# Up projection of two of three token blocks by Strassen's seven products, in a second pass over the weights

## The chip, the cores and the metric

The kernel runs on one core of a Trainium2 chip. The metric is device microseconds (us) of one execution. A core has TensorE (PE, matmuls; PEld are its weight loads), VectorE (DVE), ScalarE (ACT), GpSimd (POOL) and SyncE (SP), which here only issues transfers. TensorE accumulates into PSUM, of which the kernel uses eight tiles of 128 x 512 float32; the other engines compute on SBUF and PSUM, GpSimd on SBUF alone.

## What is computed

One step of a layer of a streaming encoder: attention, a state-space layer, then a gated feed-forward network with a causal convolution of width 3 over positions. The change touches the last part alone:

```
f, conv_state = _conv_ffn(_rmsnorm(h, g_ffn_norm), conv_hist, p)     # returned: h + f

def _conv_ffn(xn, conv_hist, p):
    up = xn @ p["w_up"]                      # (1024 + 8*16, 1024) @ (1024, 2*2816)
    full = concatenate([conv_hist, up], axis=1)
    conv = w[0] * full[:, 0:S] + w[1] * full[:, 1:S + 1] + w[2] * full[:, 2:S + 2] + p["b_dw"]
    gate, val = conv[..., :D_FF], conv[..., D_FF:]
    y = (silu(gate) * val) @ p["w_down"]     # (., 2816) @ (2816, 1024)
```

There are 1024 prompt positions and 8 running streams of 16 positions, 1152 tokens in all.

## The kernel before

Everything is held transposed: channels on the 128 partitions, tokens along the row. The 1152 tokens are three blocks of TB = 384 (b = 0, 1, 2); block 2 has the last 256 prompt tokens and the 128 tokens of the running streams. The 2816 channels of the hidden layer are NF = 22 column tiles of 128 (i), each with a gate and a value half.

Matmuls are of float32r operands (32 bit, fewer bits of mantissa). So every operand is split in a high part `h` (ScalarE, `acopy`) and a low part `l` (VectorE: source minus high part), and each product is three matmuls: hi.hi, lo.hi, hi.lo (`mm3`). One matmul has a 128x128 weight and 384 columns.

`phase_de` computes h into `hT` (all blocks, in SBUF), its norm, and the split normed input `hnh`, `hnl` of each block. Then, for every tile i and block b: `up(i, b)` accumulates gate and value in a PSUM tile `pu` each (8 x 3 matmuls); ScalarE copies `pu` to `u` and starts the convolution `c`; VectorE adds the two other taps (line 123); silu, product and split give `act`. `down(i, b, m)` multiplies `act` with one of eight 128-column pieces of the tile's `w_down` into a PSUM tile `pd`, which VectorE adds into `hT` (line 105). The downs of tile i - 1 are put one by one between the matmuls of tile i (`fill`). A weight tile (128x1024) is loaded once (`ws`), split into `wh` and `wl`, and serves all three blocks. `pu` has four PSUM tiles in turn, `pd` four.

The order of each engine's instructions is set by a scheduler that works on a model of the machine; each engine then runs its list in order. The loads stand in SP's list, also in order.

Of the kernel before, what the change touches and what calls it, by code (L numbers as in the profile page):

```python
# [72 lines left out]
SD0, SD1 = 12, 3  # L73


def build(tc, t):
# [4 lines left out]
    with root:  # L81
# [51 lines left out]
        def mm3(out, pairs, first=True, last=True):  # L133
            n = 3 * len(pairs)
            i = 0
            for (wh, wl), (xh, xl) in pairs:
                for w, x in ((wh, xh), (wl, xh), (wh, xl)):
                    nc.tensor.matmul(out, lhsT=w, rhs=x, start=first and i == 0, stop=last and i == n - 1)  # L138
                    i += 1
# [38 lines left out]
        q_dram = dram.tile([SEQ, H * QD], F32, name="q_dram")  # L178

# [1178 lines left out]
        def phase_de():  # L1358
# [4 lines left out]
            with left, right:  # L1363
                next(c_steps)
                wA = right.enter_context(tc.tile_pool(name="wA", bufs=3, side="right", **L))
# [13 lines left out]
                wB = right.enter_context(tc.tile_pool(name="wB", bufs=3, side="right", **L))  # L1379
# [42 lines left out]
                for n, closed in enumerate(c_steps):  # L1422
                    next(sd, None)
                    if closed:
                        if so is None:
                            for _ in sd:
                                pass
                            blp[2] = right.enter_context(tc.tile_pool(name="bl2", bufs=1, side="right", **L))
                            so = osteps(2)
# [17 lines left out]
                def wout(ms, b, o):  # L1447
                    pw = {}
# [19 lines left out]

                def norm(b):
# [26 lines left out]
                for n, b in enumerate(order):  # L1496
                    hload(b)
# [21 lines left out]
                def up(i, b, fill):  # L1519
                    res = []  # L1520
                    for gv in range(2):
                        hi, lo = W[i][gv]
                        f = gv * NF + i
                        w = [cv[:, f, z:z + 1] for z in range(4)]
                        p_ = psum("u", [P, TB], "pu")
                        for k in range(8):
                            mm3(p_, [((hi[:, k * P:(k + 1) * P], lo[:, k * P:(k + 1) * P]), (hn[b][0][:, k], hn[b][1][:, k]))],
                                first=k == 0, last=k == 7)
                            if k % 2 == 1:
                                fill()  # L1530
                        c = wk("M", [TB], "c")
                        nc.scalar.activation(out=c, in_=p_, func=AF.Identity, scale=w[2], bias=w[3])  # L1532
                        n = min(TB, SEQ - b * TB)
                        u = wk("M", [2 + 2 + TB + 2 * NB], "u")
                        if b == 0:
                            nc.gpsimd.memset(u[:, 0:2], 0.0)
                        else:
                            nc.gpsimd.tensor_copy(out=u[:, 0:2], in_=halo[i, gv][:, TB:TB + 2])  # L1538
                        acopy(u[:, 2:2 + n], p_[:, 0:n])
                        halo[i, gv] = u  # L1540
                        for z in (1, 0):
                            stt(c[:, 0:n], u[:, z:z + n], w[z], c[:, 0:n], ALU.mult, ALU.add)
                        if n < TB:
                            us = u[:, 2 + n:2 + n + NB * (DSEQ + 2)].rearrange("p (b s) -> p b s", b=NB)
# [42 lines left out]
                for i, b in seq:  # L1587
# [13 lines left out]
                    while todo:  # L1601
                        fill()
# [130 lines left out]
```

## Time and profile before

| | |
|---|---|
| three runs | 1546.43, 1547.09, 1541.39 us; median 1546.43 |
| profiled execution | 1542.52 us, its span 1540.5 us, instructions 23789 |
| mean granted TensorE clock | 0.973 of full speed |
| TensorE busy over the span | 1469.7 us (95%), 8733 matmuls |
| VectorE, ScalarE, GpSimd busy | 1099.0 (71%), 678.7 (44%), 324.5 us (21%) |
| transfers | 122.15 MB, mean 79 GB/s |

The span is the time from the first to the last instruction of the profiled execution; that execution took 2 us more than its span. Shares over the whole span mix the attention stages with the feed-forward stage, which takes the second half of it (from some 700 us on). In a row "x528" is a count of instructions, the number after a comma the mean duration of one in ns.

### The profile page before, as it was taken

What the parts mean: (1) busy time and instruction counts of PE and PEld (TensorE: products, weight loads), DVE (VectorE), ACT (ScalarE), POOL (GpSimd) and SP (SyncE); (2) the same over time, 40 slices, a digit from 0 to 9 for tenths busy, and PEclk for the clock granted to TensorE, in tenths of its full rate; (3) what the DMA queues carried; (4) which work ended last, traced back from release to release, by engine and by line L of the source; (5) the groups of instructions that cost most, each with busy time, mean ns of one, the idle gap of its engine ahead of it and who ended that gap; (6) DMA issues with size and microseconds to landing.
All of it is one profiled execution on the core that took longest, in us unless ns stands there. A gap on an engine that the chain in (4) does not pass through costs nothing.

```text
span 1540.5 us, 23789 instructions
## 1 busy us (share of the span) xinstructions
PE 1469.7 (95%) x8733; PEld 1415.3 (92%) x8733; DVE 1099.0 (71%) x2327; ACT 678.7 (44%) x1315; POOL 324.5 (21%) x624
## 2 busy tenths in 40 slices
PE   6989759999999999999999999999999999999998
PEld 6969647787789999999999999999999999999998
DVE  8876997575878864677676777777777677776766
ACT  6334266666567875345233333333333333333321
POOL 3271872310645221121100000000000000000000
PEclk9989859999899999999999999999999999999999
DMA  7384244733221323620121111111111111111103
GB/s 205 96 245 128 91 159 85 244 78 97 86 66 57 95 70 122 194 83 2 43 76 44 45 42 42 42 42 42 42 42 42 42 42 41 42 42 42 41 1 134
DMA packets 93460, 122.15 MB, mean 79 GB/s; under 512 B 39204, under 2 KB 73124, under 8 KB 92356
## 3 DMA queue, kind: packets, MB, share of 16 engines
q1 hardware_dynamic: 92960, 120.44, 26.1%
q8 instruction: 68, 1.11, 0.3%
q14 instruction: 48, 0.39, 0.1%
q0 software_dynamic: 384, 0.20, 0.1%
HBM read 93.95 MB, written 26.65 MB: 78 GB/s over the span
## 4 chain that ended last, share of the span: by engine, by line
PE 78%; DVE 8%; DMA 4%; POOL 4%; ACT 3%; issue 2%; SPq 1%; DVEq 0%; ACTq 0%; POOLq 0%
PE pu L138 36%; PE pd L138 17%; PE pw L138 7%; PE pk L138 2%; PE up L138 2%; POOL w L105 1%; PE pq L138 1%; PE po L1262 1%; PE psm L1217 1%; PE pst L1250 1%; PE pst L1249 1%; PE pst L1251 1%; PE po L1260 1%; PE po L1261 1%; PE pg L138 1%
## 5 line engine op out<-in xcount | busy, mean ns | idle before, releaser
L105 DVE TENSOR_TENSOR hT<-hT,pd 128x384 f32<-128x384 f32 x528 | 287.9, 550 | 218.7 <-PE pd L138 218.5
L138 PE MATMUL pu<-hnh,wh 128*128 128x384 f32 x1056 | 356.6, 338 | 0.0
L138 PE MATMUL pu<-hnl,wh 128*128 128x384 f32 x1056 | 356.4, 338 | 0.0
L138 PE MATMUL pu<-hnh,wl 128*128 128x384 f32 x1056 | 356.1, 337 | 0.0
L138 PE MATMUL pd<-act,wh 128*128 128x384 f32 x1056 | 348.7, 336 | 0.5 <-DVE hT L105 0.4
L1532 ACT ACTIVATE c<-pu,cvh 128x384 f32<-128x384 f32 x132 | 88.6, 671 | 309.8 <-PE pu L138 309.6
L138 PEld LDWEIGHTS pd<-act,wh 128*128 128x128 f32 x1056 | 197.7, 188 | 2.4 <-DVE hT L105 2.3
L138 PEld LDWEIGHTS pu<-hnh,wh 128*128 128x128 f32 x1056 | 198.4, 188 | 0.0
L138 PEld LDWEIGHTS pu<-hnl,wh 128*128 128x128 f32 x1056 | 198.3, 188 | 0.0
L138 PEld LDWEIGHTS pu<-hnh,wl 128*128 128x128 f32 x1056 | 198.0, 188 | 0.0
L123 DVE SCALAR_TENSOR_TENSOR c<-u,cvh,c 128x256 f32<-128x256 f32 (+1 forms) x352 | 171.0, 516 | 26.8 <-ACT u L102 14.2
L138 PE MATMUL pd<-act,wl 128*128 128x384 f32 x528 | 177.4, 336 | 0.0
L102 ACT ACTIVATE act<-c 128x384 fp32r<-128x384 f32 x66 | 34.7, 525 | 158.0 <-DVE c L105 158.0
L1538 POOL COPY u<-u 128x2 f32<-128x2 f32 x88 | 19.9, 227 | 384.4 <-DVE c L105 174.0
L138 PEld LDWEIGHTS pd<-act,wl 128*128 128x128 f32 x528 | 99.2, 188 | 0.0
L105 DVE TENSOR_TENSOR wl<-ws,wh 128x1024 fp32r<-128x1024 f32 x74 | 92.0, 1248 | 7.9 <-ACT wh L102 7.9
L102 ACT ACTIVATE wh<-ws 128x1024 fp32r<-128x1024 f32 x74 | 77.9, 1057 | 14.8 <-PE pw L138 8.4
L1550 POOL COPY cvo<-u 128x2 f32<-128x2 f32 x44 | 8.1, 184 | 355.2 <-ACT u L102 355.2
L1554 ACT ACTIVATE c<-c 128x384 f32<-128x384 f32 x66 | 34.6, 525 | 74.7 <-DVE c L123 74.6
L102 ACT ACTIVATE u<-pu 128x384 f32<-128x384 f32 (+2 forms) x176 | 66.3, 404 | 0.0
L138 PE MATMUL pw<-oh,wh 128*128 128x384 f32 x192 | 65.0, 340 | 0.2 <-DVE ql L123 0.2
L138 PE MATMUL pw<-oh,wl 128*128 128x384 f32 x192 | 64.4, 336 | 0.0
(461 smaller groups left out, 3088.5 us busy)
## 6 DMA issues: line engine op xcount, KB each, us to landing
ws<-in_w_up SPq DMA_DIRECT2D x44, 512.0 KB, 3.6
ws<-in_w_down SPq DMA_DIRECT2D x22, 512.0 KB, 3.7
xs<-in_xT SPq DMA_DIRECT2D x24, 192.0 KB, 3.3
os<-o_dram SPq DMA_DIRECT2D x24, 192.0 KB, 3.1
hT<-in_xT SPq DMA_DIRECT2D x24, 192.0 KB, 4.4
out_yT<-hT SPq DMA_DIRECT2D x24, 192.0 KB, 2.1
cf<-in_cT SPq DMA_DIRECT2D x8, 512.0 KB, 7.8
cn<-in_cn SPq DMA_DIRECT2D x8, 512.0 KB
```

The lines of the kernel that those rows point to most:

```text
L102: nc.scalar.activation(out=out, in_=in_, func=AF.Copy, scale=scale)
L105: (eng or nc.vector).tensor_tensor(out=out, in0=a, in1=b, op=op)
L123: nc.vector.scalar_tensor_tensor(out=out, in0=a, scalar=s, in1=b, op0=op0, op1=op1)
L138: nc.tensor.matmul(out, lhsT=w, rhs=x, start=first and i == 0, stop=last and i == n - 1)
L1217: nc.tensor.matmul(p_[:, u, 0:n], lhsT=qh[0:r, h, z * P:(z + 1) * P], rhs=kT[jj][0][0:r, 4 * g + h, 0:n], start=True, stop=True)
L1249: nc.tensor.matmul(o_, lhsT=kh[0:r, 4 * g + h, ks], rhs=qh[0:r, h, qs_], start=True, stop=False)
L1250: nc.tensor.matmul(o_, lhsT=kl[:, 4 * g + h, ks], rhs=qh[0:QD, h, qs_], start=False, stop=False)
L1251: nc.tensor.matmul(o_, lhsT=kh[0:QD, 4 * g + h, ks], rhs=ql[:, h, qs_], start=False, stop=True)
L1260: nc.tensor.matmul(po[:, qs_], lhsT=vhs, rhs=ph[:, sc_], start=f, stop=False)
L1532: nc.scalar.activation(out=c, in_=p_, func=AF.Identity, scale=w[2], bias=w[3])
L1538: nc.gpsimd.tensor_copy(out=u[:, 0:2], in_=halo[i, gv][:, TB:TB + 2])
L1554: nc.scalar.activation(out=g_, in_=g_, func=AF.Silu)
```

## The change

Blocks 1 and 2 no longer get a plain up projection. Write one tile's weights as a 2 x 2 matrix of halves, A11 and A12 for the gate (input channels 0 to 511, 512 to 1023), A21 and A22 for the value, and the normed input as B11, B21 (block 1, the two halves of the channels) and B12, B22 (block 2). The four results of A times B are eight half products; Strassen's scheme in Winograd's form needs seven, of sums of the A's (S1 to S4) and of the B's (T1 to T4), and adds the products up. Sums of the products fall partly in PSUM (three tiles per column tile, A, Y and Z: products that are needed together accumulate in one), partly on VectorE.

There are now two passes over the tiles:

- Pass 1: block 0 as before (`up1`, with its downs). Meanwhile `bsteps` reads h of blocks 1 and 2 back from a DRAM buffer `h_dram`, scales it by the norm and makes and splits the seven B operands, a step of 15 VectorE instructions of 192 columns every two tiles.
- Pass 2: `up2` computes blocks 1 and 2. The up weights are loaded and split again, as halves of 512 columns (`hw`); S1 to S4 are made first, by GpSimd (`sx`). The down weights are loaded and split again too.

In both passes the low part of every weight half is made by GpSimd (`half`). `hT` is replaced by `h0` (block 0, pass 1) and `y12` (blocks 1 and 2, loaded from `h_dram` at the start of pass 2 into space that held block 0). The downs queue in one list `todo` and run six behind (LAG). Copies of the convolution's edges, on GpSimd before, are on ScalarE in pass 2.

```diff
@@ new constants
+NX, NW, NA, NN = 8, 8, 3, 3
+AHEAD1, AHEAD2, LAG = 3, 3, 6
@@ phase_de
-                W, act, halo = {}, {}, {}
-                def loadw(i):
-                    wp = (wA, wB)[i % 2]
-                    W[i] = (wtile(t["w_up"][i], wp), wtile(t["w_up"][NF + i], wp), wtile(t["w_down"][i], wp))
...
+                def half(src):
+                    w = wpool.tile([P, 2, HW], F32R, tag="hw", name="hw", bufs=NW)
+                    split(w[:, 0], w[:, 1], src, eng=nc.gpsimd)
+                    return w
...
                 def down(i, b, m):
-                    a = act[i, b]
-                    hi, lo = W[i][2]
-                    sl = slice(m * P, (m + 1) * P)
                     p_ = psum("d", [P, TB], "pd")
-                    mm3(p_, [((hi[:, sl], lo[:, sl]), a)])
-                    y = hT[:, m, b * TB:(b + 1) * TB]
+                    mm3(p_, [(wslice(wd[b > 0, i, m // 4], m % 4), acts[i, b])])
+                    y = h0[:, m] if b == 0 else y12[0][:, m, (b - 1) * TB:b * TB]
                     add(y, y, p_)
...
+                def fill(lim=0):
+                    if len(todo) > lim:
+                        down(*todo.pop(0))
...
+                            put(B22, x2[:, 1])
+                            sub(x3[:, 0], x2[:, 0], x1[:, 0])
+                            put(T1, x3[:, 0])
+                            sub(x2[:, 1], x2[:, 1], x2[:, 0])
+                            put(T3, x2[:, 1])
...
+                PROD = (("A11", "B11", "A"), ("S2", "T2", "Y"), ("S1", "T1", "Z"), ("S3", "T3", "Y"),
+                        ("A12", "B21", "A"), ("A22", "T4", "Y"), ("S4", "B22", "Z"))
...
+                        def comb(x, a, b, op):
+                            sx[x] = wk("M", [HW], "sx")
+                            tt(sx[x], a, b, op, nc.gpsimd)
+
+                        if nm == "S2":
+                            comb("S1", a21, a22, ALU.add)
+                            comb("S2", sx["S1"], a11, ALU.subtract)
+                        elif nm == "S3":
+                            comb("S3", a11, a21, ALU.subtract)
+                        elif nm == "S4":
+                            comb("S4", a12, sx["S2"], ALU.subtract)
+                        src = {"A11": a11, "A12": a12, "A22": a22}.get(nm)
+                        ops[i, nm] = half(sx[nm] if src is None else src)
...
+                def up2(i):
+                    bank = {}
+                    fg, fv = i, NF + i
+                    for p, (a, b, x) in enumerate(PROD):
...
+                        prep2(7 * i + p + 1 + AHEAD2)
+                        if p in (1, 2):
+                            prepd(i > 0, i - 1 if i else NF - 1, p - 1)
+                        fresh = x not in bank
+                        if fresh:
+                            bank[x] = psum({"A": "y", "Y": "y", "Z": "k"}[x], [P, TB], "p" + x)
+                        p_ = bank[x]
+                        w, B = ops.pop((i, a)), bsp[b]
+                        for k in range(4):
+                            mm3(p_, [(wslice(w, k), (B[0][:, k], B[1][:, k]))], first=fresh and k == 0, last=k == 3, again=not fresh)
+                            if k % 2 == 1:
+                                fill(LAG)
+                        if p == 0:
+                            s1 = wn("s1")[:, 0:TB]
+                            acopy(s1, p_)
+                        elif p == 1:
+                            s2 = wn("s2")[:, 0:TB]
+                            add(s2, s1, p_)
+                        elif p == 3:
+                            s3 = wn("s3")[:, 0:TB]
+                            add(s3, s1, p_)
+                            uv2 = wn("uv2")
+                            csum(uv2, s3, bank["Z"], N2)
...
+                        elif p == 5:
+                            uv1 = wn("uv1")
+                            csum(uv1, s1, p_, TB)
...
+                    ug2 = wn("ug2")
+                    csum(ug2, s2, bank["Z"], N2)
```

What the change makes of the engines' lists, at three places. First GpSimd. Before, in the middle of the feed-forward stage, it has the small copies of one tile and its neighbours (`u` and `cvo`, edges of the convolution):

```order
L1550 COPY cvo<-u 128x2
L1551 COPY cvo<-u 128x16
L1536 MEMSET u 128x2 x2
L1538 COPY u<-u 128x2 x3
L1546 COPY u<-cvh 128x8x2
L1550 COPY cvo<-u 128x2
```

Now, in pass 2, one tile has these (`ws` raw weights, `sx` sums of weights, `hw` split halves):

```order
L107 TENSOR_TENSOR sx_17040<-ws_16911 128x512
L107 TENSOR_TENSOR sx_17042<-sx_17040,ws_16909 128x512
L107 TENSOR_TENSOR hw_17044<-sx_17042,hw_17044 128x512
L107 TENSOR_TENSOR hw_17092<-sx_17040,hw_17092 128x512
L107 TENSOR_TENSOR sx_17146<-ws_16909,ws_16911 128x512
L107 TENSOR_TENSOR sx_17238<-ws_16909,sx_17042 128x512
L107 TENSOR_TENSOR hw_17148<-sx_17146,hw_17148 128x512
L107 TENSOR_TENSOR hw_17178<-ws_16909,hw_17178 128x512
L107 TENSOR_TENSOR hw_17181<-ws_16913,hw_17181 128x512
L107 TENSOR_TENSOR hw_17209<-ws_16911,hw_17209 128x512
```

Thirteen full-width two-input instructions per tile (ten shown) have taken the place of the copies, and the low half of S2 (`hw_17044`) stands right behind the sum that it is made from. Second VectorE, before, near a tile's end (`hT<-hT,pd` additions of the down projection, `wl` a weight's low part, `c` the convolution):

```order
L105 TENSOR_TENSOR hT_7406<-hT_7406,pd_10846 128x384
L105 TENSOR_TENSOR wl_10479<-ws_10476,wh_10478 128x1024
L105 TENSOR_TENSOR c_10803<-c_10745,c_10803 128x384
L105 TENSOR_TENSOR hT_7406<-hT_7406,pd_10857 128x384
L105 TENSOR_TENSOR hT_7406<-hT_7406,pd_10868 128x384
L105 TENSOR_TENSOR act_10818<-c_10803,act_10818 128x384
```

And in pass 2, in the middle of a tile (`y12` stands for `hT`; `s3`, `uv1`, `uv2` are sums of products, `pY` and `pZ` their PSUM tiles, `c2` and `cg1` convolutions):

```order
L107 TENSOR_TENSOR s3_14599<-s1_14504,pY_14518 128x384
L107 TENSOR_TENSOR uv2_14601<-s3_14599,pZ_14549 128x256
L107 TENSOR_TENSOR uv2_14601<-s3_14599,pZ_14549 128x8x16
L107 TENSOR_TENSOR y12_11523<-y12_11523,pd_14583 128x384
L107 TENSOR_TENSOR y12_11523<-y12_11523,pd_14594 128x384
L125 SCALAR_TENSOR_TENSOR cg1_14629<-ug1_14631,cvh_8359,cg1_14629 128x384
L107 TENSOR_TENSOR y12_11523<-y12_11523,pd_14613 128x384
L107 TENSOR_TENSOR y12_11523<-y12_11523,pd_14624 128x384
L125 SCALAR_TENSOR_TENSOR cg1_14629<-ug1_14631,cvh_8359,cg1_14629 128x384
L107 TENSOR_TENSOR uv1_14666<-s1_14504,pY_14518 128x384
```

The weights' low parts are gone from this list, sums of products have come in between, and additions that read PSUM alternate with convolution steps whose operands are all in SBUF. Third SP's list where pass 1 ends (`h0` block 0, `ws` weights):

```order
L98 DMA ws_11583<-in_w_up 128x1024
L98 DMA ws_11585<-in_w_down 128x1024
L1550 DMA out_yT<-h0_7407 128x384 x8
L98 DMA y12_11523<-h_dram_74 128x768 x8
L98 DMA ws_11836<-in_w_up 128x1024
L98 DMA ws_11838<-in_w_up 128x1024
```

Before, SP's list had only weights there; now the stores of block 0 and the load of `y12` stand ahead of the weights of tile 2 of pass 2.

## Rows read from the trace of the kernel before

**Rows 1.** Windows: start:end length, busy PE, PEld, DVE, ACT, POOL; PEclk, DMA, GB/s.
```profile
800.00:1500.00 700.00, 700.00 (x3995) 700.00 (x3994) 488.69 (x906) 229.00 (x424) 53.28 (x221) 1.00 0.13 41
600.00:650.00 50.00, 50.00 (x315) 49.68 (x315) 23.37 (x48) 18.43 (x38) 5.70 (x6) 1.00 0.57 188
500.00:600.00 100.00, 97.50 (x813) 94.38 (x812) 72.62 (x126) 77.34 (x147) 24.76 (x19) 1.00 0.28 84
```

**Rows 2.** Waits from 800 to 1500 us: us in total, times, longest.
```profile
ACT c L1532 <- PE pu L138: 274.8, 111, 3.4
DVE hT L105 <- PE pd L138: 199.7, 277, 1.0
```

**Rows 3.** Groups of VectorE by shape: busy us, mean ns of one, idle before.
```profile
L105 DVE TENSOR_TENSOR hT<-hT,pd 128x384 f32<-128x384 f32 x528 | 287.9, 550 | 218.7 <-PE pd L138 218.5
L123 DVE SCALAR_TENSOR_TENSOR c<-u,cvh,c 128x384 f32<-128x384 f32 x176 | 108.8, 618 | 21.7 <-ACT u L102 10.4
...
L123 DVE SCALAR_TENSOR_TENSOR c<-u,cvh,c 128x256 f32<-128x256 f32 x88 | 42.4, 482 | 5.2 <-ACT u L102 3.8
...
L105 DVE TENSOR_TENSOR c<-c 128x384 f32<-128x384 f32 x66 | 36.3, 551 | 0.2
...
L123 DVE SCALAR_TENSOR_TENSOR c<-u,cvh,c 128x128 f32<-128x128 f32 x88 | 30.3, 345 | 0.0
...
L105 DVE TENSOR_TENSOR S<-pS,RK 128x264 f32<-128x264 f32 x16 | 6.5, 427 | 7.5 <-PE pS L138 7.2
```

**Rows 4.** Timeline from 688.6 us: start, us, engine, instruction.
```profile
688.70 4.94 POOL L105 TENSOR_TENSOR acc<-acc,sqh 128x384 f32<-128x384 f32 x2 [19.80 <-ACT sqh L1464]
...
689.03 1.22 DVE L105 TENSOR_TENSOR wl<-ws,wh 128x1024 fp32r<-128x1024 f32 x1
...
690.16 1.49 DVE L105 TENSOR_TENSOR hnl<-hns,hnh 128x384 fp32r<-128x384 f32 x3
...
691.57 1.47 DVE L105 TENSOR_TENSOR hT<-hT,pw 128x384 f32<-128x384 f32 x3
...
692.97 1.75 DVE L105 TENSOR_TENSOR wl<-ws,wh 128x1024 fp32r<-128x1024 f32 x1
```

**Rows 5.** Timeline of GpSimd alone from 297 us.
```profile
297.93 2.53 POOL L105 TENSOR_TENSOR wkvl<-wst,wkvh 128x512 fp32r<-128x512 f32 x2 [5.39 <-ACT wkvh L102]
```

**Rows 6.** Groups of GpSimd by shape.
```profile
L105 POOL TENSOR_TENSOR pl<-pf,ph 128x512 fp32r<-128x512 f32 x19 | 26.8, 1412 | 75.4 <-ACT ph L102 72.5 <-PE po L1261 2.9
...
L1538 POOL COPY u<-u 128x2 f32<-128x2 f32 x88 | 19.9, 227 | 384.4 <-DVE c L105 174.0 <-DVE hT L105 109.0 <-ACT u L102 96.3
...
L1536 POOL MEMSET u<- 128x2 f32 x44 | 3.0, 95 | 22.0 <-DVE hnl L105 15.1 <-DVE acc L105 4.5 <-DVE c L105 2.5
```

**Rows 7.** Timeline from 506 us, VectorE and GpSimd.
```profile
507.18 0.66 DVE L105 TENSOR_TENSOR pl<-pf,ph 128x512 fp32r<-128x512 f32 x1
...
507.23 1.77 POOL L105 TENSOR_TENSOR pl<-pf,ph 128x512 fp32r<-128x512 f32 x1 [7.26 <-ACT ph L102]
```

**Rows 8.** Groups of ScalarE by shape.
```profile
L1532 ACT ACTIVATE c<-pu,cvh 128x384 f32<-128x384 f32 x132 | 88.6, 671 | 309.8 <-PE pu L138 309.6 <-issue 0.2
...
L102 ACT ACTIVATE u<-pu 128x384 f32<-128x384 f32 x88 | 42.4, 482 | 0.0
L102 ACT ACTIVATE act<-c 128x384 fp32r<-128x384 f32 x66 | 34.7, 525 | 158.0 <-DVE c L105 158.0
...
L102 ACT ACTIVATE u<-pu 128x128 f32<-128x128 f32 x44 | 12.3, 279 | 0.0
...
L102 ACT ACTIVATE wuh<-ws 128x512 fp32r<-128x512 f32 x8 | 5.0, 629 | 2.6 <-DMA ws<-in_w_in 2.6
```

**Rows 9.** Transfers by line: count, KB each, median us from issue to landing.
```profile
ws<-in_w_up SPq DMA_DIRECT2D x44, 512.0 KB, 3.6
...
out_yT<-hT SPq DMA_DIRECT2D x24, 192.0 KB, 2.1
```

**Rows 10.** Timeline from 468.3 us, VectorE and GpSimd.
```profile
468.43 1.28 POOL L105 TENSOR_TENSOR pl<-pf,ph 128x512 fp32r<-128x512 f32 x1
...
469.13 1.00 DVE L105 TENSOR_TENSOR pl<-pf,ph 128x384 fp32r<-128x384 f32 x1
```

More of the change, by code (lines that the diff above doesn't have):

```diff
@@ L131, in split, with mm3 @@
                 stt(lo, src, scale, hi.bitcast(F32), ALU.mult, ALU.subtract)
-        def mm3(out, pairs, first=True, last=True):
+        def mm3(out, pairs, first=True, last=True, again=False):
             n = 3 * len(pairs)
@@ L137, in mm3 @@
                 for w, x in ((wh, xh), (wl, xh), (wh, xl)):
-                    nc.tensor.matmul(out, lhsT=w, rhs=x, start=first and i == 0, stop=last and i == n - 1)
+                    nc.tensor.matmul(out, lhsT=w, rhs=x, start=first and i == 0, stop=last and i == n - 1,
+                                     skip_group_check=again)
                     i += 1
@@ new lines, in gated @@
+                def gated(pool, i, b, g_, v_):
+                    nc.scalar.activation(out=g_, in_=g_, func=AF.Silu)
+                    mul(v_, g_, v_)
+                    if pool is None:
+                        a_ = wk("L", [2, TB], "act", F32R)
+                    else:
+                        a_ = pool.tile([P, 2, TB], F32R, tag="act", name="act", bufs=NA)
+                    split(a_[:, 0], a_[:, 1], v_)
+                    acts[i, b] = (a_[:, 0], a_[:, 1])
+                    todo.extend((i, b, m) for m in range(8))
@@ new lines, in phase_de, with prep1, prepd @@
+                S1 = [(n, h, i) for i in range(NF) for n in "gv" for h in range(2)]
+                halves = {}
+                pos = [0]
+                def prep1(upto):
+                    while pos[0] < min(upto, len(S1)):
+                        n, h, i = S1[pos[0]]
+                        halves[n, h, i] = half(raws[n, i][:, h * HW:(h + 1) * HW])
+                        pos[0] += 1
+                def prepd(z, i, h):
+                    if 0 <= i < NF:
+                        wd[z, i, h] = half(raws["d", i][:, h * HW:(h + 1) * HW])
@@ L1586, in phase_de @@
                     pass
[L1587 to L1606 removed]
+                xs_.close()
@@ new lines, in phase_de, with fill1 @@
+                bls.close()
+                wBs.close()
+                wAs.close()
+                bpool = right.enter_context(tc.tile_pool(name="bop", bufs=1, side="right", **L))
+                for nm in ("B11", "T2", "T1", "T3", "B21", "T4", "B22"):
+                    bsp[nm] = [bpool.tile([P, 4, TB], F32R, name=nm + "hl"[z]) for z in range(2)]
+                bs = bsteps()
+                for i in range(1, NF):
+                    skip = [LAG if i == 1 else 0]
+                    def fill1():
+                        skip[0] -= 1
+                        if skip[0] < 0:
+                            fill(LAG)
+                    up1(i, fill1, bs)
@@ new lines, in phase_de, with wn @@
+                for _ in bs:
+                    pass
+                p0s.close()
+                p2 = left.enter_context(tc.tile_pool(name="p2", bufs=1, **L))
+                yt = p2.tile([P, 8, 2 * TB], F32, name="y12")
+                for m in range(8):
+                    load(yt[:, m], h_dram[:, m])
+                y12.append(yt)
+                def wn(name):
+                    n = 2 + 2 + TB + 2 * NB
+                    if name in ("s1", "s2", "uv2"):
+                        return p2.tile([P, n], F32, tag="n", name=name, bufs=NN)
+                    return wk("M", [n], name)
@@ L1608, in rope @@
+                raw("g", 0)
+                raw("v", 0)
+                prep2(AHEAD2)
+                for i in range(NF):
+                    up2(i)
+                for h in range(2):
+                    prepd(True, NF - 1, h)
+                store(t["conv_out"], cvo)
+                while todo:
+                    fill()
         def rope(pool, out, x, c, s, tag, eng=None):
```

262 lines of the change are left out of this document (175 added, 87 removed).

## The prediction

> **What bounds the kernel now.** Read the table by stretch first [rows 1]. Between 800 and 1500 us TensorE is busy 700.00 of 700 us at a granted clock of 1.00, VectorE 488.69 (70%), ScalarE 229.00 (33%), GpSimd 53.28 (8%). Then read who waits for whom in that stretch [rows 2]: ScalarE and VectorE wait for TensorE's groups (274.8 and 199.7 us in total) and no row has TensorE waiting. So the up and down projections cost what their matmuls cost, and every other engine has slack. 3995 matmuls in 700 us make 0.1752 us each [rows 1]; one of the 22 column tiles (i in the code) has 216 of them, 37.8 us, and 22 tiles make 833 of the span's 1540.5 us. The pace is a start-to-start pace: the 337 ns of one matmul on the page overlaps its neighbour's.
>
> **What the change takes away.** Per tile, blocks 1 and 2 took 2 x 2 x 8 x 3 = 96 up matmuls; seven products of 4 x 3 are 84. 12 x 22 = 264 matmuls of unchanged shape go: 264 x 0.1752 = 46.3 us. Nothing else leaves TensorE. Per tile, pass 1 now has 48 + 24 = 72 matmuls (12.6 us) and pass 2 84 + 48 = 132 (23.1 us). The gain comes only if the other engines keep these two paces, which leave them less time per tile than 37.8 us, with more work.
>
> **What it adds, engine by engine, per tile.**
>
> VectorE, pass 2: 16 additions of `pd` into y at 0.550, 3 more of that shape (s2, s3, uv1), convolution 4 x 0.618 + 4 x 0.482 + 4 x 0.345, gating 4 x 0.55 [rows 3]. The two sums that end in a strided part (uv2, ug2) do not occur before; by the 264-column sum out of PSUM (0.427) and the 128-column row (0.345) I take 0.78 each. Sum 20.0 us of 23.1. Instructions that queue back to back overlap a little: three such additions took 1.47 us at 691.57 [rows 4], 0.06 less each, so the lower bound is 17.8.
>
> VectorE, pass 1: 8 x 0.55, 4 x 0.618, 2 x 0.55, that is 8.0, and in the first 16 tiles half a step of the operand combinations each, 7.5 instructions of 192 columns. That width is not in the trace; between 0.345 (128) and 0.482 (256) I take 0.41. Sum 11.1 of 12.6, by the same overlap 9.8 at least.
>
> GpSimd gets the low halves of all weights, which were VectorE's (`wl<-ws,wh`): 6 subtractions of 128x512 in pass 1, 9 in pass 2 and 4 weight sums, 418 in all. Back to back, two such took 2.53 us [rows 5], 1.26 each; in the attention stretch, where VectorE is busy, the mean was 1.412 [rows 6]; the worst I use is 1.77 [rows 7]. Pass 1: 6 x 1.412 + 0.6 for copies and memsets [rows 6] = 9.1 of 12.6. Pass 2: 16.4, 18.4 or 23.0 of 23.1, and some 0.8 us where S2's low half waits for ScalarE's high half of it (0.629 [rows 8]). Its small copies of pass 2 go to ScalarE.
>
> ScalarE, pass 2: 9 halves at 0.629, 4 x 0.525, 2 x 0.482, 0.671, 0.525, the two-part starts 1.3, and 11 small copies, which I bound by 0.279 [rows 8]: 14.3 of 23.1. Pass 1: 8.3 of 12.6. Neither bounds.
>
> Transfers: three weights of 0.52 MB per 12.6 us are 125 GB/s in pass 1, 68 in pass 2. From 600 to 650 us the queues moved 188 GB/s while TensorE was busy all the time [rows 1]. A weight lands 3.6 us after its issue [rows 9] and is issued a tile ahead: cover enough, I cost it at nothing; uncovered it would be 3.6 us a tile.
>
> **The handover.** On SP's queue the load of y12 (3.1 MB) stands behind the eight stores of block 0, and tile 2's weights stand behind it. A store takes 2.1 us to land [rows 9], 3.1 MB at 188 GB/s 16.7 us, the first weight 3.6, its split about 2: 24.4 us. In TensorE's list 136 matmuls stand between the last `pd` of block 0 and the first that needs those weights, 23.8 us. Between nothing (if the queues move faster than in that stretch) and 5 us (if the split waits for its engine); I take 3. At the front the norms of blocks 1 and 2 get lighter, but TensorE was full there, so nothing comes of it.
>
> **The term that decides: VectorE and GpSimd together.** At 468.43 a GpSimd subtraction began; VectorE's `pl` of 384 columns, begun 0.70 us later, took 1.00 instead of 0.55. At 507.23 it was GpSimd that came 0.05 us after VectorE's `pl`, and took 1.77. Two `acc` of 384 columns, narrower than the 1.26 us ones, took 4.94 us together from 688.70, while VectorE ran one `wl`, three `hnl` and another `wl`; but the three `hT<-hT,pw` there, which read PSUM, ran at their pace of 1.47 [rows 3, 4, 7, 10]. So the trace shows that two instructions with two operands in SBUF each, one on either engine, take turns, and that an addition out of PSUM does not. In pass 2, 16 of VectorE's 39 instructions per tile are of the first kind, in about ten runs (counted in its order of one tile). GpSimd is at work for 18.4 of 23.1 us, 79%, so the first of a run waits on average half a subtraction with that chance: 10 x 0.63 x 0.79 = 5.0 us. VectorE then needs 22.8 to 25.0 us where TensorE needs 23.1. In pass 1 GpSimd is at work 72% and there are about 8 runs: 3.6 us, 13.4 to 14.7 against 12.6 in 16 tiles. What queues behind a blocked instruction is the next additions of `pd`; those free the four `pd` buffers, and after four downs TensorE stands.
>
> The Trainium skill says the same more strictly (SBUF — State Buffer, "Who interferes with whom"): a tensor-tensor instruction of VectorE with both inputs in SBUF and a GpSimd instruction that reads SBUF exclude each other for the whole instruction, and whoever starts first holds the port. By that rule, with every wait as above, this would be the first rival below, 1575. The trace agrees as to the turns; that a second VectorE instruction may slip through in a run (the `hnl`) it shows too.
>
> I take for pass 2 0.8 us per tile, near the middle of 22.8 to 25.0 less 23.1, 18 us; for pass 1 0.6 in 16 tiles, 10 us, under its lower bound of 0.8, since the runs there are short and between additions. For scale: from 500 to 600 us, with VectorE at 73% and ScalarE at 77%, TensorE lost 2.5% [rows 1]; 28 us of 785 is 3.6%.
>
> **Sum.** 1542.5 (profiled) - 46.3 + 10 + 18 + 3 = 1527. The three runs have their median at 1546.4, 3.9 above the profiled one; I forecast 1530, between 1527 and 1531. The clock stays: it was granted in full (1.00, which is 2.4 GHz) in all three stretches, also where TensorE was 97.5% busy [rows 1].
>
> **Rivals.**
> 1. *The port decides (slower).* VectorE at its upper bounds: 25.0 - 23.1 = 1.9 in 22 tiles, 14.7 - 12.6 = 2.1 in 16: 42 + 34 + 3 - 46.3 = +33, 1575. If the followers in a run wait too (6 x 1.26 x 0.79 = 6 us more a tile), it goes past 1650. It ends on that side once pass 2 takes over 24.6 us a tile with pass 1 as forecast ((46.3 - 13) / 22 = 1.5 over). For it: the `pl` and `acc` rows; against: the additions out of PSUM, over half of VectorE's work, are free of it. 0.29.
> 2. *GpSimd feeds too late.* At 1.77 each and 0.8 of waiting, 23.8 to 24.6 us a tile in pass 2, TensorE waits for low halves (0.7 to 1.5, 15 to 33 us) beside pass 1's 10 and the 3: 1524 to 1542, 1540 at its likeliest, since GpSimd looks ahead by three halves only. For it: TensorE's order has several high-half matmuls drawn ahead of low ones. Against: the mean was 1.412, not 1.77. 0.17.
> 3. *Nothing given back.* VectorE's overlap and short runs hold the pace: 1542.5 - 46.3 + 3 = 1499. Against: four engines at 60 to 100%, each in a fixed order. 0.13.
> 4. The forecast, 1515 to 1538: 0.41.
>
> **Chances.** 0.5% of 1546.4 is 7.7 us, about what a measurement of this kernel can tell from no change: under 1538.7 is faster, over 1554.2 slower. Faster: 0.13 + 0.38 + 0.05 = 0.56. Same: 0.03 + 0.10 + 0.02 = 0.15. Slower: 0.29. Range 1500 to 1582: below it the clean case's lower half, above it the rest of the first rival. The forecast's own range is 1515 to 1538.
>
> **What the trace after would show.** 264 matmuls fewer at the same 0.175 us. Windows of pass 1 and pass 2: tiles of 13.2 and 23.9 us, TensorE busy 95 to 97%, waits of TensorE under `pd` for VectorE. Right: VectorE's two-input rows longer than before (`c2`, `act`), its y12 rows at 0.55; GpSimd's `hw` rows near 1.4. Rival 1: TensorE waits for VectorE over 70 us in sum, VectorE over 95% busy. Rival 2: TensorE's longest waits end with GpSimd's `hw`. Wrong altogether: a stall at the handover over 10 us, or a clock under 1.00 in pass 1 or 2.

## The result, and the profile after

The changed kernel takes 1595.31 us (median of 4 runs, 1595.27 to 1598.05) against 1546.68 for the kernel before: ratio 1.033, 95% interval 1.030 to 1.035. It is slower by 3.3%, outside the range of the prediction (1500 to 1582), on the side that had 0.29. Its profiled execution took 1598.05 us, its span is 1596.2: 55.7 longer than the profiled one before. The medians differ by 48.6; what follows accounts for the two profiled executions.

The table by stretch of the kernel after, which answers to [rows 1] (start:end, length, then busy time and instructions of PE, PEld, DVE, ACT, POOL; granted clock, DMA share, GB/s). Pass 1 runs up to 1008 us, pass 2 from 1015:

```profile
600.00:700.00 100.00, 96.44 (x581) 94.81 (x580) 47.17 (x91) 35.23 (x72) 25.44 (x22) 1.00 0.48 151
700.00:1008.00 308.00, 285.83 (x1579) 277.20 (x1578) 261.04 (x421) 148.92 (x312) 182.89 (x209) 0.98 0.39 122
750.00:950.00 200.00, 183.05 (x1002) 175.69 (x1002) 187.00 (x298) 101.00 (x218) 123.33 (x138) 0.98 0.38 118
1008.00:1100.00 92.00, 79.23 (x406) 75.43 (x405) 65.02 (x110) 40.68 (x104) 61.40 (x48) 0.93 0.35 118
1100.00:1400.00 300.00, 282.71 (x1561) 278.00 (x1560) 271.76 (x462) 136.78 (x376) 214.24 (x154) 0.97 0.21 64
1100.00:1500.00 400.00, 376.82 (x2078) 370.82 (x2077) 361.02 (x614) 182.26 (x501) 286.77 (x206) 0.97 0.21 64
```

The pace of an undisturbed matmul is 0.1752 us [rows 1]; what a stretch is longer than its matmuls at that pace is TensorE's loss in it. 1579 matmuls are worth 276.6 us, so the 308 us of pass 1 lose 31.4. The handover (1008 to 1100 us, the first tiles of pass 2 included) loses 92 - 71.1 = 20.9, the 400 us of pass 2 lose 400 - 364.1 = 35.9. The same count gives 8.5 us for the rest of pass 2 and 4.9 up to 700 us, beyond what was lost before (28 matmuls fewer by then, 26 of them from 600 us on, where before has 607). In sum 101.6, less the 46.3 of the 264 matmuls: 55.3 of the 55.7. From now on a tile's length is worked out in the same way: pass 1 has 72 matmuls a tile, 72 x 200 / 1002 = 14.4 us (12.6 at full pace); pass 2 has 132, 132 x 300 / 1561 = 25.4 us (23.1).

Who waits for whom, TensorE's rows from 705 to 1008 and from 1014 to 1592 us (us in total, times, longest); before, TensorE had no row [rows 2]:

```profile
PE pd L140 <- DVE h L107: 9.8, 6, 3.1
PE pu L140 <- POOL hw L107: 3.9, 3, 2.1
PE pu L140 <- ACT hw L104: 3.5, 3, 2.4
PE pu L140 <- POOL u L1647: 2.8, 3, 1.0
```
```profile
PE pd L140 <- DVE y L107: 27.8, 22, 1.9
PE pY L140 <- DVE s L107: 7.2, 4, 2.9
PE pA L140 <- ACT hw L104: 2.5, 1, 2.5
```

In pass 2 most of the waiting is for VectorE. In pass 1 it is not: 9.8 us are for VectorE, 12.2 for halves of weights (4.8 for ScalarE's high ones with a row of 1.3 under `pd`, 4.6 for GpSimd's low ones with one of 0.7, and the 2.8 of the last row, where GpSimd's tiny memset of `u` stands right behind a low half).

The groups of VectorE and GpSimd by shape, 1100 to 1400 us (busy us, mean ns), beside [rows 3, 6]. In the rows, names stand without their digits: `ug`, `uv` are the summed products in SBUF, `cg` and `c` their convolution, `hw` the weight halves, `sx` the weight sums, `s` s1 to s3:

```profile
L107 DVE TENSOR_TENSOR y<-y,pd 128x384 f32<-128x384 f32 x191 | 99.3, 547 | 16.6 <-PE pd L140 16.3
L125 DVE SCALAR_TENSOR_TENSOR c<-ug,cvh,c 128x128 f32<-128x128 f32 x24 | 33.2, 1381 | 0.0
L107 DVE TENSOR_TENSOR act<-c,act 128x384 fp32r<-128x384 f32 x24 | 27.7, 1154 | 4.4 <-ACT act L104 3.6
L125 DVE SCALAR_TENSOR_TENSOR c<-ug,cvh,c 128x256 f32<-128x256 f32 x23 | 22.7, 986 | 0.0
L125 DVE SCALAR_TENSOR_TENSOR cg<-ug,cvh,cg 128x384 f32<-128x384 f32 x24 | 19.2, 799 | 0.1
...
L125 DVE SCALAR_TENSOR_TENSOR c<-uv,cvh,c 128x384 f32<-128x384 f32 x24 | 14.6, 610 | 0.0
```
```profile
L107 POOL TENSOR_TENSOR hw<-ws,hw 128x512 fp32r<-128x512 f32 x60 | 86.3, 1461 | 1.6 <-ACT hw L104 1.6
```

The additions that read PSUM kept their 0.55 us. Of the instructions with two operands in SBUF those that fall beside GpSimd's halves took up to four times as long (0.345 to 1.381), and those that fall in a pause of GpSimd (`c<-uv` of 384) kept 0.61. The place is the same in each tile. VectorE, GpSimd and TensorE around it in one tile (start, us):

```profile
1305.57 0.54 DVE L107 TENSOR_TENSOR y<-y,pd 128x384 f32<-128x384 f32 x1
1306.04 1.19 DVE L107 TENSOR_TENSOR act<-c,act 128x384 fp32r<-128x384 f32 x1
1307.14 2.80 DVE L125 SCALAR_TENSOR_TENSOR c<-ug,cvh,c 128x256 f32<-128x256 f32 x2
1309.87 0.54 DVE L107 TENSOR_TENSOR y<-y,pd 128x384 f32<-128x384 f32 x1
```
```profile
1305.45 5.64 POOL L107 TENSOR_TENSOR hw<-ws,hw 128x512 fp32r<-128x512 f32 x4
```
```profile
1309.03 0.34 PE L140 MATMUL pA<-B21h,hw 128*128 128x384 f32 x1
1310.46 0.44 PE L140 MATMUL pd<-act,hw 128*128 128x384 f32 x1 [1.09 <-DVE y L107]
```

GpSimd runs four halves without a pause, 1.41 us each. VectorE's addition out of PSUM at 1305.57 passes in 0.54; then `act` and two `c` take 3.9 us in place of some 1.4 (e1, below), one of them for each half of GpSimd's. Behind them is the addition that frees a `pd`; TensorE stands for it for 1.09 us, until 1310.46.

### The profile page after: what moved, and what is told of

It reads as the page before. It is cut to its first block, busy times and chain, and to the rows that moved or that the text cites. A ratio compares the mean times of both kernels' runs of the same rounds, so it can differ in the third digit from the quotient of the medians.

```text
span 1596.2 us, 24730 instructions
## 1 busy us (share of the span) xinstructions
PE 1456.4 (91%) x8469; PEld 1380.4 (86%) x8469; DVE 1273.8 (80%) x2503; ACT 808.9 (51%) x1817; POOL 849.6 (53%) x866
## 4 chain that ended last, share of the span: by engine, by line
PE 50%; DVE 23%; DMA 7%; POOL 7%; issue 7%; ACT 5%; SPq 1%; DVEq 0%; POOLq 0%; ACTq 0%
PE pd L140 11%; DVE c L125 8%; PE pY L140 7%; PE pu L140 6%; PE pA L140 4%; DVE y L107 3%; PE pw L140 3%; POOL hw L107 3%; PE pk L140 2%; PE up L140 2%; PE pZ L140 2%; DVE h L107 1%; POOL w L107 1%; PE pq L140 1%; DMA ws<-in_w_down 1%
## 5 line engine op out<-in xcount | busy, mean ns | idle before, releaser
L107 POOL TENSOR_TENSOR hw<-ws,hw 128x512 fp32r<-128x512 f32 x242 | 341.2, 1435 | 72.9 <-ACT hw L104 67.3
L140 PE MATMUL pd<-act,hw 128*128 128x384 f32 x1584 | 341.3, 343 | 42.4 <-DVE y L107 27.8
L140 PEld LDWEIGHTS pd<-act,hw 128*128 128x128 f32 x1584 | 283.4, 191 | 58.5 <-DVE y L107 36.6
L107 DVE TENSOR_TENSOR y<-y,pd 128x384 f32<-128x384 f32 x352 | 181.7, 546 | 27.9 <-PE pd L140 27.6
L140 PE MATMUL pu<-hnh,hw 128*128 128x384 f32 x704 | 189.0, 341 | 10.3 <-POOL hw L107 3.9
L107 POOL TENSOR_TENSOR hw<-sx,hw 128x512 fp32r<-128x512 f32 x88 | 126.3, 1447 | 63.4 <-ACT hw L104 63.1
L104 ACT ACTIVATE hw<-ws 128x512 fp32r<-128x512 f32 x242 | 137.0, 619 | 17.8 <-DMA ws<-in_w_up 10.1
L140 PEld LDWEIGHTS pu<-hnh,hw 128*128 128x128 f32 x704 | 130.1, 191 | 14.3 <-ACT hw L104 5.5
L140 PE MATMUL pu<-hnl,hw 128*128 128x384 f32 x352 | 119.4, 340 | 0.0
L125 DVE SCALAR_TENSOR_TENSOR c<-ug,cvh,c 128x256 f32<-128x256 f32 (+1 forms) x88 | 97.6, 1144 | 0.0
L1567 ACT ACTIVATE c<-c 128x384 f32<-128x384 f32 x44 | 23.1, 525 | 114.3 <-DVE c L125 114.2
```

The source lines that it names most:

```text
L104: nc.scalar.activation(out=out, in_=in_, func=AF.Copy, scale=scale)
L107: (eng or nc.vector).tensor_tensor(out=out, in0=a, in1=b, op=op)
L125: nc.vector.scalar_tensor_tensor(out=out, in0=a, scalar=s, in1=b, op0=op0, op1=op1)
L1567: nc.scalar.activation(out=g_, in_=g_, func=AF.Silu)
```

## Experiments

Theory A: GpSimd's long instructions hold up VectorE's instructions with two operands in SBUF, the additions of `pd` queue behind them, and TensorE stands without a free one. Theory B: VectorE's own work and its order are too long for the shorter tile. All ratios are to the kernel before, with 95% intervals; tile lengths are worked out from the windows 750:950 and 1100:1400 as above.

**e1: no subtraction on GpSimd.**

```diff
-                    split(w[:, 0], w[:, 1], src, eng=nc.gpsimd)
+                    acopy(w, src.rearrange("p (o k) -> p o k", o=1).to_broadcast([P, 2, HW]))
```

> The low halves are no longer a subtraction on GpSimd: one ScalarE instruction writes the source into both parts of a half, so that the low part is here a second copy of the source (that part of the computation is changed). TensorE's instructions stay as they are. Theory A (GpSimd's subtractions hold up VectorE's two-input instructions, VectorE then frees the pd buffers late): VectorE's c and act rows fall back to 0.345 to 0.62 us, pass 2 goes from 25.5 to 23.1 to 23.6 us a tile, pass 1 from 14.2 to 12.6 to 13.2, the half-speed stretches of TensorE's clock become rarer; total 1500 to 1530. Theory B (VectorE's own work and the fixed order of a tile are too long, without GpSimd): pass 2 stays at 25 or above, pass 1 at 13.8 or above; total over 1570.

The kernel leaves the subtraction out: the low part is a second copy of the source, made by ScalarE, and TensorE's instructions stay. 1511.61 us, 0.979 (0.978 to 0.981). Windows, and VectorE's groups from 1100 to 1400 us:

```profile
750.00:950.00 200.00, 199.36 (x1142) 197.44 (x1141) 146.08 (x327) 150.89 (x241) 7.91 (x64) 1.00 0.43 139
1100.00:1400.00 300.00, 300.00 (x1726) 300.00 (x1725) 243.71 (x510) 203.50 (x416) 68.38 (x53) 1.00 0.21 69
```
```profile
L125 DVE SCALAR_TENSOR_TENSOR c<-uv,cvh,c 128x256 f32<-128x256 f32 x27 | 24.0, 890 | 0.0
L107 DVE TENSOR_TENSOR c<-c,c 128x384 f32<-128x384 f32 x13 | 16.8, 1295 | 40.0 <-ACT c L1567 40.0
...
L107 DVE TENSOR_TENSOR act<-c,act 128x384 fp32r<-128x384 f32 x26 | 14.1, 544 | 0.0
L125 DVE SCALAR_TENSOR_TENSOR c<-ug,cvh,c 128x256 f32<-128x256 f32 x26 | 12.2, 470 | 0.0
...
L125 DVE SCALAR_TENSOR_TENSOR c<-ug,cvh,c 128x128 f32<-128x128 f32 x26 | 8.7, 336 | 0.0
```

Pass 2 is at 22.9 us a tile, pass 1 at 12.6: TensorE full, the clock 1.00. The rows of `c<-ug`, `cg` and `act` that had grown are back at the durations of [rows 3]. Two others have grown instead, `c<-c,c` to 1.295 and `c<-uv` of 256 to 0.890 (0.745 and 0.605 in the changed kernel): they now fall beside the weight sums that GpSimd still makes. Theory A holds by its own numbers, B falls: the Strassen pass does run at TensorE's pace when the low halves don't stand in VectorE's way. By itself e1 doesn't tell A from low halves that come too late, since it makes them early as well; e4 and f1, which leave them on GpSimd, bear on that.

**e2: the subtractions on VectorE.** `split(w[:, 0], w[:, 1], src)`, without `eng=nc.gpsimd`.

> The low halves are subtracted on VectorE, as in the kernel before; GpSimd keeps only S1 to S4 and the small copies. Theory A: VectorE loses its waits but gains 9 subtractions a tile at about 0.67 us in pass 2 and 6 in pass 1: 20.0 + 6.0 = 26.0 us a tile in pass 2 and 11.1 + 4.0 = 15.1 in pass 1, so VectorE is full: pass 2 at 26, pass 1 at 15, total 1600 to 1640. Theory B (the waits cost little, VectorE's own 20 us and their order make 25.5): pass 2 goes up by the whole 6.0, to 30 us or more; total over 1680.

1556.70 us, 1.009 (1.007 to 1.010): both theories' totals were too high.

```profile
1100.00:1400.00 300.00, 285.29 (x1593) 274.51 (x1592) 300.00 (x578) 147.29 (x387) 67.63 (x49) 1.00 0.22 65
```

VectorE is full (300.00 of 300) and the tile takes 24.9 us, not 26.0: VectorE's own work had been put too high. In e1 it is busy 243.71 / 300 x 22.9 = 18.6 us a tile, waits beside the sums included, where the prediction had 20.0 (17.8 by its lower bound). The striking thing is the comparison with the changed kernel: with 9 more instructions a tile and no pause left, VectorE gives a shorter tile (24.9) than in the changed kernel, where it is busy 91% (25.4). All of that difference can be the clock, 1.00 here and 0.97 there (last section): the stands of TensorE are more but shorter.

**e3: the same work of GpSimd in shorter pieces.**

```diff
+                    for z in range(0, HW, HW // 2):
+                        sub(w[:, 1, z:z + HW // 2], src[:, z:z + HW // 2], w[:, 0, z:z + HW // 2], nc.gpsimd)
...
-                            tt(sx[x], a, b, op, nc.gpsimd)
+                            for z in range(0, HW, HW // 2):
+                                tt(sx[x][:, z:z + HW // 2], a[:, z:z + HW // 2], b[:, z:z + HW // 2], op, nc.gpsimd)
```

> GpSimd does the same subtractions and weight sums in two pieces of 256 columns each. Theory A with turns at the end of an instruction: a VectorE instruction that finds GpSimd at work waits half as long; if GpSimd's pieces take 0.7 us each, pass 2 goes from 25.5 to 24.3 to 25.0 us a tile, VectorE's 256-column c out of ug from 1.00 to under 0.8; total 1565 to 1585. Rival C (the two engines share a rate, so that the length of an instruction does not matter, or GpSimd itself is the bound): no gain, or slower by the fixed cost of 18 more GpSimd instructions a tile; total 1590 to 1630.

1549.94 us, 1.004 (1.002 to 1.006): 45 us back, more than by A's numbers (1565 to 1585). Part of it is the clock, 1.00 where the changed kernel had 0.97.

```profile
1100.00:1400.00 300.00, 292.99 (x1642) 283.40 (x1640) 268.88 (x489) 144.92 (x398) 256.92 (x322) 1.00 0.21 64
```
```profile
L125 DVE SCALAR_TENSOR_TENSOR c<-ug,cvh,c 128x128 f32<-128x128 f32 x26 | 21.4, 824 | 0.0
```
```profile
L107 POOL TENSOR_TENSOR hw<-ws,hw 128x256 fp32r<-128x256 f32 x123 | 101.3, 855 | 0.0
```

GpSimd is busy longer (256.92 against 214.24 of 300 us), two pieces taking 1.71 us where one took 1.46, and the tile is still 1.3 us shorter, at 24.1. So rival C (a shared rate, or GpSimd's supply) falls; it is how long one instruction holds the other up that counts: `c<-ug` of 128 fell from 1.381 to 0.824.

**e4: pass 1's convolution out of PSUM.**

```diff
-                        acopy(u[:, 2:2 + TB], p_)
-                        nc.gpsimd.tensor_copy(out=hal[:, f], in_=u[:, TB:TB + 2])
-                        conv(c, u, f, TB)
+                        acopy(hal[:, f], p_[:, TB - 2:TB])
+                        for z in (1, 0):
+                            stt(c[:, 2 - z:TB], p_[:, 0:TB - 2 + z], cv[:, f, z:z + 1], c[:, 2 - z:TB], ALU.mult, ALU.add)
```

> Pass 1's convolution reads the up projection out of PSUM, without the copy u in SBUF: its four instructions a tile have then one operand in SBUF. Theory A: they keep about 0.6 us (0.93 in the changed kernel) and free pd earlier; pass 1 goes from 14.2 to 13.0 to 13.6 us in the 16 tiles with combinations of the operands; total lower by 8 to 20 us, pass 2 unchanged at 25.5. Theory B (load and order): the pu buffers are held longer, pass 1 the same or slower, total 1590 to 1605.

1572.08 us, 1.019 (1.016 to 1.022): 23 us less. The convolution's steps beside GpSimd's halves, from 750 to 950 us, in the changed kernel and in this one:

```profile
L125 DVE SCALAR_TENSOR_TENSOR c<-u,cvh,c 128x384 f32<-128x384 f32 x56 | 52.5, 938 | 1.8 <-ACT u L104 1.4
```
```profile
L125 DVE SCALAR_TENSOR_TENSOR c<-pu,cvh,c 128x382 f32<-128x382 f32 x30 | 18.3, 610 | 0.4
```
```profile
750.00:950.00 200.00, 195.79 (x1105) 190.52 (x1104) 179.24 (x317) 101.86 (x236) 124.97 (x93) 1.00 0.44 134
```

Moving one operand to PSUM takes the wait away, with GpSimd's subtractions as before: pass 1 goes from 14.4 to 13.0 us a tile, pass 2 stays at 25.4, as theory A has it. The edit also takes out GpSimd's memset and copy and ScalarE's wide copy `u`, and in this window TensorE's waits for VectorE fell from 9.2 to 2.9 us and those for halves of weights from 7.7 to 1.3. How much of pass 1's loss was each by itself is not separated.

**f1: PSUM operands in both passes.** e4, and in pass 2 the gate and value of block 1 are convolved where they lie, in their PSUM tiles (a bank is one):

```diff
-                            ug1 = wn("ug1")
-                            acopy(ug1[:, 2:2 + TB], p_)
+                            ug1 = u_        # the bank, [P, 2 + TB]; p_ = u_[:, 2:2 + TB]
...
-                            uv1 = wn("uv1")
+                            uv1 = u_
```

> Subtractions in whole 512-column pieces, as in the changed kernel. Pass 1's convolution reads PSUM as in e4; in pass 2 the gate of block 1 is convolved straight out of the pA bank, and the value of block 1 is summed in place in the pY bank and convolved from there, so that 4 of VectorE's 16 instructions a tile with two operands in SBUF have one in PSUM; ScalarE's copy of 384 columns goes. Theory A: these four fall to 0.62 us, pass 2 goes from 25.5 to 24.3 to 25.0 us a tile; total 1545 to 1565. Theory B (order and load, or banks that are now held longer): TensorE waits under pA or pY, pass 2 at 25.5 or above; total 1572 or more.

1558.60 us, 1.009 (1.007 to 1.011).

```profile
1100.00:1400.00 300.00, 289.46 (x1621) 279.84 (x1620) 283.88 (x475) 141.10 (x379) 221.41 (x161) 1.00 0.21 64
```
```profile
L125 DVE SCALAR_TENSOR_TENSOR c<-uv,cvh,c 128x256 f32<-128x256 f32 x26 | 39.4, 1514 | 0.0
...
L125 DVE SCALAR_TENSOR_TENSOR cg<-pA,cvh,cg 128x384 f32<-128x384 f32 x24 | 14.7, 612 | 0.0
L125 DVE SCALAR_TENSOR_TENSOR c<-pY,cvh,c 128x384 f32<-128x384 f32 x24 | 14.5, 605 | 0.0
```

The rows that read PSUM are at 0.61, and the wait moves to the next of the other kind (`c<-uv` of 256, 0.605 before, now 1.514). VectorE's busy time per tile hardly changed (23.0 to 23.1 us), yet the tile fell to 24.4: the waits stand at places where they reach TensorE less (it waits 9.0 us for `y`, 0.8 at the longest, where the changed kernel has 16.6 and 1.9), and the clock stays at 1.00.

**f2, f3, f4: remedies together.** f2 is f1 with e3's pieces. f3 is e3 and e4, and `half(..., nc.vector if nm in ("S2", "A12", "A22") else None)` in pass 2, with which VectorE makes three of the seven products' low halves. f4 is f2 with two of them (A12, A22) on VectorE.

> The same with GpSimd's instructions in pieces of 256 columns. Theory A: both remedies add up in part; pass 1 12.7 to 13.2, pass 2 from 24.1 to 23.3 to 23.9 us a tile; total 1520 to 1537. Theory C (GpSimd at 21 us a tile is itself the bound of pass 2): pass 2 stays at 24.1; total 1538 to 1545.

> Pieces of 256 columns, pass 1's convolution out of PSUM, and in pass 2 the low halves of three of the seven products (S2, A12, A22) by VectorE. Theory A: GpSimd is at work for some 16 us a tile, VectorE gains 2.0 us of its own and loses about as much waiting; pass 2 23.3 to 23.9; total 1522 to 1537. Theory B: the 2.0 us come on top, pass 2 at 25 or more; total over 1555.

> Pieces of 256 columns, the PSUM operands of f1 in both passes, and the low halves of two products (A12, A22) by VectorE. Theory A: pass 2 23.0 to 23.5, pass 1 12.7 to 13.2, nearly the clean kernel; total 1510 to 1527. Theory C: pass 2 stays near 24; total 1535 to 1545.

f2: 1525.02 us, 0.988 (0.986 to 0.989), pass 2 at 23.4 us a tile. f3: 1518.87 us, 0.984 (0.982 to 0.986), 23.1. f4: 1525.61 us, 0.988 (0.986 to 0.990), 23.4. All three are within A's bounds or a little better, C falls again (f2), and the remedies don't add up: f4 is no better than f2. f3, which has GpSimd's least work (218 of 300 us busy; f2 258, f4 237) and no PSUM operands in pass 2, is the best. Pass 1 is at 12.6 in all three. Windows of f3:

```profile
1100.00:1400.00 300.00, 299.10 (x1712) 297.51 (x1711) 289.29 (x547) 153.84 (x414) 218.01 (x258) 1.00 0.22 69
```

VectorE is busy 96% here and TensorE 99.7%.

**b1: the kernel before, with GpSimd's low halves alone.** `split(hi, lo, s, eng=nc.gpsimd)` for the up and down weights, 1024 columns each.

> The kernel before, with one part of the change alone: the low halves of the up and down weights are subtracted on GpSimd, 1024 columns in one instruction, three a tile of 37.8 us. Theory A: VectorE's instructions with two operands in SBUF wait here too (some rows longer than 0.62 us), but VectorE has some 11 us of slack a tile, so TensorE stays busy all the time: 1535 to 1552, no difference. Rival: a hold of over 2 us is felt at once, since four pd buffers cover no more than 2 us: 1560 or more.

1550.63 us, 1.005 (1.003 to 1.007): at the edge of what can be told, within A's bounds. The profiled execution is the shortest of its six, 1544.79.

```profile
800.00:1500.00 700.00, 700.00 (x3994) 700.00 (x3994) 462.75 (x851) 227.66 (x427) 191.50 (x280) 1.00 0.13 41
```
```profile
L105 DVE TENSOR_TENSOR c<-c 128x384 f32<-128x384 f32 x55 | 60.0, 1091 | 0.0
```

`c<-c` waits here too (1.091; 0.551 in [rows 3]), and TensorE stays busy all the time from 800 to 1500 us: there the wait costs nothing, since VectorE, busy 66%, has the time to catch up. Between 700 and 800 us TensorE does wait once for VectorE's `hT`, 2.0 us, and the profiled execution is 14 matmuls behind by 800 us, its whole 2.5 us; where the rest of the median's 7 us went is not shown. GpSimd is at work for 27% of the time here and for 71% in pass 2, so this is the milder case: the move of the low halves by itself didn't cost 3%; more of them, in a tile that leaves no slack, did.

**f6 and f7: the handover.** f6 is f3 with `raw("g", 0); raw("v", 0)` ahead of the loads of `y12`; f7 is f3 with these two and `prep2(AHEAD2)` inside pass 1's last tile, ahead of its value half.

> The kernel of f3 with the first two weight loads of pass 2 issued on SP's queue ahead of the eight loads of y12 instead of behind them. Theory H (the prediction's handover: the weights stand behind 3.1 MB): the stall of 2.5 to 5 us at the start of pass 2 goes, total lower than f3 by 3 to 6 us, ratio to before 0.980 to 0.982. Rival: the stall is the end of pass 1's list on ScalarE or the y12 data itself, and the time stays at f3's, 0.983 to 0.985.

> The kernel of f3 with the first three halves of pass 2 (A11, S2, S1 with their weight sums) issued within the last tile of pass 1: on ScalarE they stand ahead of that tile's last act instead of behind it. Theory H2 (the handover's stall is ScalarE's order: the first half of pass 2 queues behind act, which waits for VectorE's last gating product): TensorE's gaps under pA and pY at the start of pass 2, 2.8, 0.8 and 2.5 us in f3, go to under 1.5 us in sum; total lower than f3's by 3 to 6 us, ratio to before 0.980 to 0.982. Rival (pass 1's last tile is late itself, and the wait only changes its name): the first tile of pass 2 takes 24 us as in f3; ratio 0.983 to 0.986.

f6: 1520.35 us, 0.985 (0.984 to 0.987), no different from f3. SP's list is the same in both, these weights stood ahead of `y12` already, so f6 tells nothing of the queue. f7: 1510.22 us, 0.979 (0.978 to 0.981), some 8 us below f3 and the best kernel of this study. ScalarE around the handover, f3 first, then f7:

```profile
978.07 0.16 ACT L104 ACTIVATE hal<-pu 128x2 f32<-128x2 f32 x1
982.45 0.52 ACT L104 ACTIVATE act<-c 128x384 fp32r<-128x384 f32 x1 [4.21 <-DVE c L107]
982.87 0.61 ACT L104 ACTIVATE hw<-ws 128x512 fp32r<-128x512 f32 x1
```
```profile
978.09 1.15 ACT L104 ACTIVATE hw<-sx 128x512 fp32r<-128x512 f32 x2 [2.59 <-POOL sx L107]
...
984.30 0.53 ACT L104 ACTIVATE act<-c 128x384 fp32r<-128x384 f32 x1 [2.88 <-DVE c L107]
```

In f3 the first half of pass 2 queues behind an `act` that waits 4.21 us for VectorE's product; in f7 it runs ahead of it. TensorE's waits for ScalarE's `hw` between 960 and 1000 us (2.4 under `pA`, 2.1 under `pY` in f3) are gone in f7. That is theory H2 (ScalarE's order), with a gain above its 3 to 6 us: in f3 the granted clock was 0.50 from some 983 to 987 and from 990 to 994 us, right behind these two waits, and in f7 it was 1.00 all through.

## Why the prediction was wrong, by its own steps

- **What goes.** Right: 264 matmuls fewer (8469 left), at the same 0.175 us where nothing waits: e1's 1726 in 300 us.
- **VectorE takes turns with GpSimd.** Right in kind, and the term of the wait nearly in size: the excess of VectorE's rows over the least durations (e1's, or those of [rows 3]) adds up to some 5.9 us a tile (two `c<-ug` of 128 by 1.05, two of 256 by 0.52, two `act` by 0.61, two `cg` by 0.19, the rest 1.1), where the prediction had 5.0. Its assumption that only the first of a run waits was wrong: in the rows from 1306.04 each of three waits for a half of its own. That its own work was put at 20.0 and measured 18.6 or less made up for it: VectorE is busy 271.76 / 300 x 25.4 = 23.0 us a tile, at the low end of its 22.8 to 25.0.
- **The step that failed: from VectorE's need to the tile's length.** "I take for pass 2 0.8 us per tile" set the excess as VectorE's need less TensorE's 23.1. With 23.0 of need the excess should have been nothing; it was 2.3 us a tile. In pass 1 0.6 us was taken, "under its lower bound"; VectorE was busy 187.00 of 200 us, 13.4 us a tile, and the tile took 14.4, 1.8 over. So the term of 18 us measured 44.4 (35.9 and 8.5), that of 10 us 31.4. A sum over the tile doesn't see that the waits fall on one place, with four `pd` buffers as the only cover, and that what VectorE then has free (it waits 16.3 us for `pd` later) comes too late. That VectorE's busy time doesn't set the tile's length f1 and e2 show from both sides: the same busy time with a shorter tile, and a longer one with a shorter tile (there by the clock). In pass 1 late halves of weights had a part as well.
- **"The clock stays."** Wrong. From 1100 to 1400 us the granted clock was 0.97; that cost 0.5 to 0.6 of the 2.3 us a tile (last section).
- **The handover at 3 us.** 20.9, first tiles of pass 2 included. With the clock this is one of the prediction's two signs of "wrong altogether", and both came. It was not the queue that the prediction costed (`y12` ahead of weights): no wait of TensorE ends with a transfer there. It waited 6.5 us under `pY` for VectorE's `s`, most of it twice 2.9 us behind a run of `c` and `act` in which steps took 1.2 to 1.5 us beside GpSimd, so by the same turns; 3.8 us for ScalarE's `hw`, by the order that f7 undid in f3; 1.8 us for GpSimd's `hw`; and the granted clock was 0.93. At the front, costed at nothing, 4.9 us went by 700 us; TensorE waited 1.7 us for VectorE's `hx`, 1.5 for ScalarE's `R` and 0.3 for VectorE's `acc` there, and why these came late stays open.
- **Transfers at nothing; GpSimd's pace.** Right: no wait of TensorE ends with a transfer in either pass, and `hw` took 1.46 where 1.412 was taken. TensorE's waits for GpSimd's halves (rival 2) are 4.6 us in pass 1, 7.4 with those put down to the memset behind them, and 1.8 later, in sum.
- **The rivals.** Rival 1 has the mechanism and the side, and its 1575 is 20 us short: pass 2 at its upper bound (25.0, measured 25.4), pass 1 within (14.7, 14.4), the rest is the handover and the front. Its signs were set wrong: TensorE's waits for VectorE sum to 45 us, not 70, and VectorE is 91% busy, not 95. A full VectorE was not needed. Its "past 1650" for followers that wait too was far too much: they do wait, and all waits of a tile sum to 5.9 us, not 11.

The Trainium skill (SBUF — State Buffer, "SBUF: two separate sides") says that of a VectorE instruction with two SBUF inputs and a GpSimd instruction that reads SBUF the one that starts first has the shared ports for the whole instruction while the other fully blocks. The trace agrees, in its followers (three instructions, three halves) and in PSUM operands being free of it (0.612 in f1, 0.610 in e4). The Trainium skill (Perfetto Trace Analysis, "Optimizing Scalar/DVE Operations") says that where ScalarE or VectorE is not saturated but causes bubbles on other engines, breaking up instructions may let work finish sooner. e3 agrees, though the instructions that it broke up are GpSimd's: 45 us.

## What to carry to other kernels

When an edit shortens the bound engine's stage, don't compare other engines' sums with the new length alone: look for the longest run of instructions that can be held up in one place, and ask whether the buffers behind it (here four `pd`) last that long. An engine that helps another can cost more by the length of one instruction than by its share of time: pieces of 256 columns, more work in all, were worth 45 us. With short pieces, PSUM operands, some halves on VectorE and the first halves of pass 2 issued early, the seven products are 2.1% faster than the plain ones (f7).

## What the runs showed of the hardware

The clock fell after long stands of TensorE. From 1130 to 1570 us of the changed kernel a stand of 1.85 to 1.91 us and one of 1.09 or 1.10 alternate from tile to tile, nine of each. Behind eight of the nine long ones the granted clock fell to its lower level, behind the one at 1386 us and behind all the short ones it didn't. Windows around one that fell, at its stand and behind it:

```profile
1333.00:1337.00 4.00, 2.15 (x12) 1.83 (x11) 3.73 (x5) 1.80 (x5) 3.99 (x4) 1.00 0.68 176
1337.20:1340.60 3.40, 3.40 (x12) 3.40 (x12) 1.80 (x3) 0.10 (x1) 3.40 (x3) 0.50 0.68 237
```

After the stand of 1.85 us the granted clock was 0.50 (1.2 GHz) for 3.4 us, with 12 matmuls where full speed has 19, some 1.3 us lost. From 1100 to 1400 us there are five such stretches, 6.5 us in 11.8 tiles, beside 17.3 us of stands. In e2, e3 and f1, where the waits for `y` are at most 0.9 us long (1.9 in the changed kernel), the clock from 1100 to 1400 us is 1.00, in e2 in spite of one wait of 1.67 us for a half. So here it fell with the long stands, though not with each, and added to their cost. The kernel before had no stand over 0.2 us from 600 to 1535 us. What decides whether it falls stays open.
